# Broadcast and score products on all 128 rows of the array instead of 32 or 64, in a two-layer SSD / attention / gMLP block

## The chip, the cores and the metric

The kernel runs on one core of one Trainium2 chip. The metric is the device time of one execution in microseconds, lower is better. The kernel before was run three times: 1681.04, 1684.17 and 1684.0 us, median 1684.0 us.

## The reference, cut to what matters

Two layers work on 256 context tokens and 256 latent tokens of 1024 features. Each layer makes one wide input projection and feeds three branches with it: a bidirectional state space scan (SSD, 16 heads in four groups), an attention (8 heads of 64) and a gated MLP over tokens. Their gated sum goes through an output projection, and a SwiGLU FFN follows. The second layer computes the context only as far as the latents need it. The two places that matter here:

```python
seg = a_cum[:, :, :, None] - a_cum[:, :, None, :]
decay_ls = jnp.exp(jnp.where(tri, seg, -jnp.inf))
...
q, k = rmsnorm(q, q_norm), rmsnorm(k, k_norm)
s = jnp.einsum('bqhd,bkhd->bhqk', q, k) * (Dh ** -0.5)
```

So each SSD head needs, for each of two directions, a matrix of differences of cumulated decays between tokens, and each attention head needs scores of normalized q and k.

## The kernel before, in words

All products are made with float32 operands cut into a high part in the short TensorE format (F32R) and a low part that holds the rest. A product of a weight with activations is three TensorE products, high by high, high by low, low by high (`mm3`, line 250). `gemm` (line 255) makes one tile of 128 features that way, 24 products for 1024 input features. Weights stream from memory in tiles of 128 x 1024; ScalarE (ACT) makes the high part (line 226) and VectorE (DVE) the low part (line 236), at most two tiles ahead of TensorE (`LA`, line 41).

The order of all work is written by hand. `tick` (line 314) is called by the products with weights and lets the side work of three queues go on: the SSD's (`ssd`), attention's and the MLP's (`att`), and the conditioning vectors' (`mod`). Each `yield` in a side generator is a place where the products with weights go on. TensorE takes its instructions in that order. PSUM has eight banks of 512 columns (`S`, line 119), and 61 buffers of 128 x 512 serve nearly all intermediate tiles (`T`, line 116).

The places that the change touches:

- `decay` (line 902). For one head, one stream and each direction, a product spreads one row of `R` over all partitions: the stationary operand is a column of `sel` (minus one where the row index is the wanted one), repeated 128 times. `R` has 128 rows: for each of the two streams 64, namely the high parts of two directions times 16 heads and then their low parts. The product takes only the 64 rows of its own stream (`p`, line 905) and 384 columns. A second product (line 910) adds a mask in bfloat16 with the identity `idb` as stationary operand and `mfb` moving, on 128 rows. A call makes two such pairs.
- `carried` (line 952). For a pair of heads, a product with `selp` spreads rows of `RA` over 64 partitions each; it takes 32 rows, those of the group, and 512 columns.
- `qk_norm` (line 1008). The inverse norms `RQ` of the heads are spread in the same way, 32 rows for each of four pairs of heads (line 1035).
- `product` (line 1071). The scores of one head are two products: `Q` (high part of q, twice, one above the other) with `K` (high and low part of k), on 128 rows, and `lo` (low part of q) with the high part of k, on the head's own 64 rows.
- `stack` (line 1044) prepares Q, K and `lo` of a head, at least one step of `attention` before its scores.
- The constants: `cst`, `sel`, `selp`, `mfb` (lines 129 to 150, 608 to 619).

```python
p = slice(0, 64) if last else slice(64 * s_, 64 * s_ + 64)
mm(ps[:, 0:384], sel[p, d * 16 + hd:d * 16 + hd + 1].to_broadcast([64, 128]),
   Rt["R"][p, (128, 0)[d]:(512, 384)[d]], True, False)
...
mm(pa, selp[32 * g:32 * g + 32, pr].rearrange("k a b -> k (a b)"), Rt["A"][32 * g:32 * g + 32, :])
...
mm(ps, Q[:, q0:q0 + 128], K[:, 0:n], True, False)
mm(ps, lo[p, q0:q0 + 128], K[p, 0:n], False, True)
```

Of the kernel before, what the change touches and what calls it, by code (L numbers as in the profile page):

```python
# [9 lines left out]
F32 = mybir.dt.float32  # L10
# [15 lines left out]
# columns of the parameter pack  # L26
# [3 lines left out]
# columns of the constant pack  # L30
C_GT, C_LE, C_LT, C_GE, C_ONE, C_ID, C_MF, C_MB = (128 * i for i in range(8))
C_COS = 1024
C_SIN = 1280
C_ROW = 1536
C_BS = 1568
C_SP = 1600
NC_ = 1604
# [58 lines left out]
def kernel(ctx: ExitStack, tc: tile.TileContext, a, out):  # L96
# [31 lines left out]
    # ------------------------------------------------------------------ constants  # L128
    cst = cpool.tile([128, NC_], F32, name="cst")
    csil = cpool.tile([128, 2, D], F32, name="csil")  # L130
    csT = cpool.tile([128, 8, 32], F32, name="csT")
# [9 lines left out]
    epsb = cpool.tile([128, 1], F32, name="epsb")  # L141
    DVE.memset(epsb, EPS)
    eps4 = cpool.tile([128, 1], F32, name="eps4")
    DVE.memset(eps4, 4.0 * EPS)
    eps64 = cpool.tile([128, 1], F32, name="eps64")
    DVE.memset(eps64, 64.0 * EPS)
    idb = cpool.tile([128, 128], BF16, name="idb")
    mfb = cpool.tile([128, 256], BF16, name="mfb")
    sel = cpool.tile([128, 32], F32R, name="sel")
    selp = cpool.tile([128, 2, 2, 64], F32R, name="selp")  # L150
# [7 lines left out]
    # ------------------------------------------------------------------ adaLN vectors  # L158
# [22 lines left out]
    def mod_gen(items):  # L181
        """items: (layer, group of eight feature tiles, both streams)"""
# [23 lines left out]
    # ------------------------------------------------------------------ weight stream  # L206
# [48 lines left out]
    def gemm(acts, c0, c1=512, la=LA):  # L255
        """one tile of 128 features"""
        nk = len(acts)
        ps = S("g")
        for k, (ah, al, b) in enumerate(acts):
            wh, wl = ws.get(pos[0] + k, la=la)  # L260
            mm3(ps[:, c0:c1], wh, wl, ah[:, c0 - b:c1 - b], al[:, c0 - b:c1 - b], k == 0, k == nk - 1)
            if k % KT == KT - 1 or k == nk - 1:
                tick((k % KT + 1) / 4 * (c1 - c0) / 512)
        pos[0] += nk
        return ps

    def gemm_group(acts, nk, n, ranges, kmajor, pl=None, tk=True):
        """n tiles of 128 features, k outside, one range of tokens after the other"""
# [13 lines left out]
    # ------------------------------------------------------------------ side work  # L282
# [19 lines left out]
    def later(dt, fn):  # L302
        """emits fn when the tensor engine has been given dt more"""
        if dt:
            pending.append((now[0] + dt, fn))
        else:
            fn()
# [6 lines left out]
    def tick(f=1.0):  # L314
        """f: share of twelve passes over 512 tokens that the tensor engine has just been given"""
# [29 lines left out]
    def table(func):  # L345
        """loads the function's table ahead of its use"""
        ACT.activation(dummy, epsb, func)

    # ------------------------------------------------------------------ norms over features
    class SumSq:  # L350
# [21 lines left out]
        def root(self, c0, c1, scale, bias):  # L372
            """1 / sqrt(scale * sum + bias), with tokens on partitions"""
# [9 lines left out]
        def spread(self, c0, c1):  # L383
            """... and on all partitions (in PSUM)"""
# [6 lines left out]
    class MakeH:  # L391
        """the modulated norm of one range of tokens, one tile after the other; hi and lo start at column b"""
# [4 lines left out]
        def to(self, k):  # L397
            """emits all tiles up to k"""
# [20 lines left out]
    class Scaled:  # L419
        """the latents of x times A with the shift as two more columns: products with it need no norm yet"""  # L420
# [27 lines left out]
        def norm(self, ps):  # L448
            """(product without the shift's part, the shift's part)"""
# [5 lines left out]
    # ------------------------------------------------------------------ start  # L455
# [7 lines left out]
    for i0, i1 in ((C_ONE, C_MF), (C_ROW, C_BS)):  # L463
        SP.dma_start(out=cst[:, i0:i1], in_=a["cst"][:, i0:i1])
# [27 lines left out]
    def start_rows(k):  # L492
        """shift and scale of 128 features"""
# [9 lines left out]
    def start_mod(k):  # L503
        """... with features on partitions, and h of these features"""
# [16 lines left out]
    # the first product runs along, its operands' features outside  # L521
# [38 lines left out]
    x = None  # L560
# [6 lines left out]
    # ================================================================== layers  # L567
    for l in range(NL):
# [8 lines left out]
        # tanh(x / 2) stands for the sigmoids  # L577
        DVE.tensor_scalar(pcol(P_BG, 120), pcol(P_BG, 120), 0.5, None, MUL)

        # ---------------- gMLP: u with features on partitions, v with tokens on partitions  # L580
# [27 lines left out]
        if not last:  # L608
            SP.dma_start(out=cst[:, 0:C_ONE], in_=a["cst"][:, 0:C_ONE])
            SP.dma_start(out=cst[:, C_MF:C_ROW], in_=a["cst"][:, C_MF:C_ROW])  # L610
            SP.dma_start(out=cst[:, C_BS:NC_], in_=a["cst"][:, C_BS:NC_])
            DVE.tensor_copy(idb, ident)
            DVE.tensor_copy(mfb, cst[:, C_MF:C_MF + 256])
            DVE.tensor_scalar(sel, cst[:, C_ROW:C_ROW + 32], -1.0, None, MUL)
            DVE.tensor_copy(selp, cst[:, C_SP:C_SP + 4].rearrange("p (a b) -> p a b", a=2).unsqueeze(3).to_broadcast(
                [128, 2, 2, 64]))
            # -1 where the rows of lo are
# [3 lines left out]
        def token_major(n0, evac, between=()):  # L621
            """256 columns of the projection with tokens on partitions; others' tiles between"""
# [44 lines left out]
        # ---------------- convolution: B 8..11, C 12..15, xs 0..7  # L667
        Bt, Ct, xs = [], [], []

        def conv(ps, m, b0):  # L670
            """half of the five taps' sum, then silu; m: tile of the convolution's channels"""
# [43 lines left out]
        def dt_gemm():  # L715
            """four column tiles at once, each with a quarter of the features"""
# [17 lines left out]
        Rt = {}  # L734

        def dt_gen():
# [18 lines left out]
            # log1p(e) = 2 atanh(e / (2 + e))  # L755
# [19 lines left out]
            # by token: sums over the tokens of a tile that follow or precede, and over all of them  # L775
# [10 lines left out]
            # -F and -G of each token, relative to the middle of the sequence: [tile, stream, twice, direction, head]  # L786
            s0 = 1 if last else 0
            for i in (0, 1):
# [3 lines left out]
            # decays to the context's ends  # L792
# [4 lines left out]
            # decays from the context's ends to the latents: [direction, tile, (group, twice, head, -)]  # L797
# [15 lines left out]
            # by row: hi of direction and head, then lo; each tile of tokens twice  # L813
            ps, pa = S(), S()
            m = 64 if last else 128
            for i in (0, 1):
                PE.transpose(ps[0:m, i * 128:i * 128 + 128],
                             nF[:, i, s0:].rearrange("p s r d h -> p (s r d h)"), ident)
# [6 lines left out]
            ACT.copy(R4[0:m], twice(ps[:, 0:256], slice(0, m)))  # L825
            ACT.copy(RA, pa)
            yield
            for p0 in range(32, m, 64):
# [6 lines left out]
        # ---------------- SSD, one group of four heads at a time  # L835
# [9 lines left out]
        def ssd_group(g):  # L845
            streams = (1,) if last else (0, 1)
            xa, xb = xs[2 * g], xs[2 * g + 1]
            # context: tokens on partitions, x (256 columns) and B (128)
# [28 lines left out]
            # the context's end states  # L877
# [24 lines left out]
            def decay(s_, hh):  # L902
                """exp(F_l - F_s) and exp(G_l - G_s) of one head, masked: [s0 l0 | s0 l1 | s1 l1], [s0 l0 | s1 l0 | s1 l1]"""
                hd = 4 * g + hh
                p = slice(0, 64) if last else slice(64 * s_, 64 * s_ + 64)
                pf, pb = S(), S()
                for d, ps in ((0, pf), (1, pb)):
                    mm(ps[:, 0:384], sel[p, d * 16 + hd:d * 16 + hd + 1].to_broadcast([64, 128]),
                       Rt["R"][p, (128, 0)[d]:(512, 384)[d]], True, False)
# [10 lines left out]
            def weights(s_, hd, ef, eb):  # L920
                """W[s, l] of one head, both directions"""
# [5 lines left out]
                # s in tile 0  # L927
                STT(W[:, 128:256], ef[:, 128:256], df(0), c[:, 128:256], MUL, MUL)
                DVE.tensor_scalar(eb[:, 0:128], eb[:, 0:128], db(0), None, MUL)
                # s in tile 1  # L930
# [8 lines left out]
            def yout(s_, pr, W, ex):  # L939
                """y of a pair of heads, in the place of xs"""  # L940
# [11 lines left out]
            def carried(pr):  # L952
                """what the context's end states add to the latents of a pair of heads"""
                pa, pc = S(), S()
                mm(pa, selp[32 * g:32 * g + 32, pr].rearrange("k a b -> k (a b)"), Rt["A"][32 * g:32 * g + 32, :])
# [35 lines left out]
        # ---------------- q and k, attention  # L991
# [3 lines left out]
        def qk_tile(j, kind):  # L995
            """j: pair of heads"""
# [11 lines left out]
        def qk_norm(kind):  # L1008
            """one over the root of each head's mean square; q's with the scores' factor of 1/8"""
# [17 lines left out]
            # rows of hi, then of lo  # L1027
# [4 lines left out]
            for j in range(4):  # L1032
                ps = S()
                p = slice(32 * j, 32 * j + 32)
                mm(ps[:, b:], selp[p, 0].rearrange("k a b -> k (a b)"), RQ[p, b:])
# [5 lines left out]
        def attention():  # L1041
            st = {}

            def stack(hd):
                """hi of q twice, hi over lo of k (or lo over hi), and lo of q"""
# [4 lines left out]
                st[hd] = Q, lo, K, p  # L1050
# [20 lines left out]
            def product(ps, hd, q0, n):  # L1071
                Q, lo, K, p = st[hd]
                mm(ps, Q[:, q0:q0 + 128], K[:, 0:n], True, False)
                mm(ps, lo[p, q0:q0 + 128], K[p, 0:n], False, True)
# [44 lines left out]
            def transp(s_, pr):  # L1119
                """P with keys on partitions: [key, key tile, query]"""  # L1120
# [59 lines left out]
        def vg_half(half):  # L1180
            def ev(i, o):
# [4 lines left out]
                elif last:  # L1186
                    # the context's h, for the tiles that follow
# [19 lines left out]
        # ---------------- convolution of one group, other tiles while the group's arithmetic goes on  # L1207
# [23 lines left out]
        # ---------------- gated branches  # L1231
# [17 lines left out]
        def gated_branch(br, acts, first, lag, ready=None, done=None):  # L1249
            """gate tiles, and branch tiles lag behind them"""  # L1250
# [15 lines left out]
        # ---------------- gate and norm of the SSD branch  # L1266
# [10 lines left out]
        def ssd_norm():  # L1277
            yield
            yield
            # z carries a factor of two  # L1280
# [18 lines left out]
        # ---------------- projection of the SSD branch  # L1299
# [14 lines left out]
        # ---------------- output projection and residual  # L1314
# [309 lines left out]
```

## Time and profile before

| | before |
|---|---|
| median of three runs (1681.04 to 1684.17) | 1684.0 us |
| span of the profiled execution, first to last instruction | 1679.5 us |
| the profiled execution's own time | not told apart from the three; 1.5 to 4.7 us above the span by them |
| TensorE busy (products) | 1668.5 us, 99% of the span |
| VectorE busy | 1161.1 us, 69% |
| ScalarE busy | 789.9 us, 47% |
| GpSimd busy | 0.2 us |
| granted TensorE clock, mean | 0.996 of full speed |

How to read the rows: PE is TensorE's product, PEld its load of the stationary operand, DVE VectorE, ACT ScalarE, POOL GpSimd. `s<-R,sel` names the tile written, then the moving and the stationary operand; `64*128 64x384` is 64 rows by 128 columns of the array and 384 moving columns. Ends of products are modelled, so a duration of 0.39 us says little; the distance from one start to the next tells how fast TensorE goes. Products of plain float32 operands (for instance `state`, `W`, `pt`) appear as two instructions each.

### The profile page before, as it was taken

What the parts mean: (1) busy time and instruction counts of PE and PEld (TensorE: products, weight loads), DVE (VectorE), ACT (ScalarE), POOL (GpSimd) and SP (SyncE); (2) the same over time, 40 slices, a digit from 0 to 9 for tenths busy, and PEclk for the clock granted to TensorE, in tenths of its full rate; (3) what the DMA queues carried; (4) which work ended last, traced back from release to release, by engine and by line L of the source; (5) the groups of instructions that cost most, each with busy time, mean ns of one, the idle gap of its engine ahead of it and who ended that gap; (6) DMA issues with size and microseconds to landing.
All of it is one profiled execution on the core that took longest, in us unless ns stands there. A gap on an engine that the chain in (4) does not pass through costs nothing.

```text
span 1679.5 us, 24795 instructions
## 1 busy us (share of the span) xinstructions
PE 1668.5 (99%) x9578; PEld 1378.1 (82%) x9578; DVE 1161.1 (69%) x2206; ACT 789.9 (47%) x1411; POOL 0.2 (0%) x4
## 2 busy tenths in 40 slices
PE   8999999999999999999999999999999999999999
PEld 5877677767678888888888888887777889999999
DVE  4377788768785865676666655778887887686553
ACT  3456554544653323432222212657455685465442
POOL 0000000000000000000000000000000000000000
PEclk8999999999999999999999999999999999999999
DMA  9412111123233445444556775433222345645553
GB/s 360 152 63 90 62 51 64 51 88 126 82 107 125 151 148 178 145 149 165 165 167 203 253 241 181 162 100 101 76 76 100 110 144 173 209 156 189 188 171 132
DMA packets 77157, 237.45 MB, mean 141 GB/s; under 512 B 9072, under 2 KB 17008, under 8 KB 76912
## 3 DMA queue, kind: packets, MB, share of 16 engines
q1 hardware_dynamic: 77040, 235.88, 41.9%
q8 instruction: 75, 1.23, 0.3%
q14 instruction: 42, 0.34, 0.1%
HBM read 231.65 MB, written 4.19 MB: 140 GB/s over the span
## 4 chain that ended last, share of the span: by engine, by line
PE 93%; DVE 3%; DMA 2%; ACT 1%; issue 1%; SPq 0%; DVEq 0%; ACTq 0%
PE g L126 77%; PE s L126 13%; DMA wm<-in_wmod 1%; PE s L1128 1%; DVE lo L236 1%; ACT hi L226 1%; DVE scr L196 0%; DMA x<-in_xT 0%; PE s L855 0%; PE rs L126 0%; DMA pv<-in_pv 0%; DVE xbc L682 0%; DVE xm L1330 0%; PE s L863 0%; SPq L461 0%
## 5 line engine op out<-in xcount | busy, mean ns | idle before, releaser
L126 PE MATMUL g<-hh,hi 128*128 128x512 f32 (+1 forms) x1280 | 474.6, 371 | 0.0
L126 PE MATMUL g<-hl,hi 128*128 128x512 f32 (+1 forms) x1280 | 461.7, 361 | 0.0
L126 PE MATMUL g<-hh,lo 128*128 128x512 f32 (+1 forms) x1280 | 461.6, 361 | 0.0
L236 DVE TENSOR_TENSOR lo<-wr,hi 128x1024 fp32r<-128x1024 f32 x316 | 381.3, 1219 | 100.9 <-ACT hi L226 100.7
L226 ACT CAST hi<-wr 128x1024 fp32r<-128x1024 f32 x316 | 322.5, 1046 | 37.8 <-DMA wr<-in_ws 34.9
L126 PEld LDWEIGHTS g<-hh,hi 128*128 128x128 f32 x1280 | 241.9, 189 | 51.6 <-issue 14.6
L126 PEld LDWEIGHTS g<-hh,lo 128*128 128x128 f32 x1280 | 241.6, 189 | 37.3
L126 PEld LDWEIGHTS g<-hl,hi 128*128 128x128 f32 x1280 | 241.9, 189 | 34.4 <-DVE hl L410 0.3
L196 DVE SCALAR_TENSOR_TENSOR scr<-wm,csil 128x1024 bf16<-128x1024 f32 x128 | 156.2, 1220 | 57.2 <-DMA wm<-in_wmod 57.1
L126 PE MATMUL g<-hp,hi 128*128 128x256 f32 x608 | 109.5, 283 | 0.0
L682 DVE SCALAR_TENSOR_TENSOR xbc<-g,pv,xbc 128x508 f32<-128x508 f32 (+3 forms) x128 | 91.3, 713 | 13.3 <-ACT xbc L676 10.1
L126 PEld LDWEIGHTS g<-hp,hi 128*128 128x128 f32 x608 | 94.8, 192 | 0.0
L126 PE MATMUL g<-hp,lo 128*128 128x256 f32 x304 | 86.2, 284 | 0.8 <-DVE lo L236 0.8
L1237 ACT ACTIVATE th<-g,pv 128x512 f32<-128x512 f32 (+1 forms) x48 | 28.0, 582 | 102.3 <-PE g L126 99.4
L126 PE MATMUL g<-fh,lo 128*128 128x512 f32 x176 | 68.6, 390 | 0.6 <-DVE lo L236 0.6
L126 PE MATMUL g<-fl,hi 128*128 128x512 f32 x176 | 68.5, 389 | 0.0
L126 PE MATMUL g<-fh,hi 128*128 128x512 f32 x176 | 68.5, 389 | 0.0
L337 ACT CAST fh<-f 128x512 fp32r<-128x512 f32 x22 | 13.6, 620 | 112.4 <-DVE f L1387 112.4
L126 PE MATMUL g<-hi,hh 128*128 128x256 f32 x224 | 64.7, 289 | 0.2 <-ACT hi L226 0.2
L126 PE MATMUL g<-lo,hh 128*128 128x256 f32 x224 | 63.6, 284 | 1.1 <-DVE lo L236 1.1
L1387 DVE TENSOR_TENSOR f<-s,g 128x256 f32<-128x256 f32 (+1 forms) x41 | 22.6, 551 | 60.7 <-PE g L126 60.3
L126 PE MATMUL g<-fp,hi 128*128 128x256 f32 x352 | 63.4, 283 | 0.0
(321 smaller groups left out, 2811.9 us busy)
## 6 DMA issues: line engine op xcount, KB each, us to landing
wr<-in_ws SPq DMA_DIRECT2D x316, 512.0 KB, 3.9
wm<-in_wmod SPq DMA_DIRECT2D x80, 512.0 KB, 4.3
wm<-in_wm SPq DMA_DIRECT2D x32, 256.0 KB, 5.8
bias<-in_rpb SPq DMA_DIRECT2D x32, 128.0 KB, 2.1
x<-in_xT SPq DMA_DIRECT2D x8, 256.0 KB, 5.2
xm<-in_xT SPq DMA_DIRECT2D x8, 256.0 KB, 6.0
xmid<-xm SPq DMA_DIRECT2D x8, 256.0 KB, 4.6
xr<-xmid SPq DMA_DIRECT2D x8, 256.0 KB, 5.3
```

The lines of the kernel that those rows point to most:

```text
L126: PE.matmul(o, l, r, start=start, stop=stop)
L196: DVE.scalar_tensor_tensor(scr, raws[n], 1.0, csil[:, v, :], MUL, MUL, accum_out=modr[l][:, ft, v:v + 1])
L226: ACT.copy(hi, self.raw[i])
L236: DVE.tensor_tensor(lo, self.raw.pop(i), hi, SUB)
L337: ACT.copy(hi, src[:, c0:])
L682: DVE.scalar_tensor_tensor(av3[:, :, o0:o1], pv3[:, :, o0 + d:o1 + d], w(j), av3[:, :, o0:o1], MUL, ADD)
L1128: PE.transpose(ps[:, kt * 256 + qt * 128:kt * 256 + qt * 128 + 128], src, ident)
L1237: ACT.activation(th[:, c0:], ps[:, c0:], AF.Tanh, scale=0.5, bias=pcol(P_BG + br * 8 + m))
L1387: DVE.tensor_tensor(t[:, r0:r1], s[:, r0:r1], pb[:, r0:r1], MUL)
```

## The change

The products with 32 or 64 rows take all 128 rows; zeros in the stationary operand stand for the rows that aren't wanted. For that, `sel` gets 64 columns (a half for each stream), `selp` 8 x 128 columns, `lo` is filled with zeros in the other half of its rows by GpSimd, and the second layer's `nF` is filled with zeros for the stream that it lacks, so that its transposes and `R` have 128 rows too. Some constants move: the masks to a tile of the general buffers, the transposed conditioning vectors `csT` too, and three small constants into one tile. Comments are removed in many places. The diff, cut to what acts:

```diff
-    csT = cpool.tile([128, 8, 32], F32, name="csT")
+    csT = T("csT")[:, 0:256].rearrange("p (k v) -> p k v", v=32)
...
-    sel = cpool.tile([128, 32], F32R, name="sel")
-    selp = cpool.tile([128, 2, 2, 64], F32R, name="selp")
+    sel = cpool.tile([128, 64], F32R, name="sel")
+    selp = cpool.tile([128, 8, 128], F32R, name="selp")
...
-            SP.dma_start(out=cst[:, C_MF:C_ROW], in_=a["cst"][:, C_MF:C_ROW])
-            SP.dma_start(out=cst[:, C_BS:NC_], in_=a["cst"][:, C_BS:NC_])
+            SP.dma_start(out=cst[:, C_COS:C_ROW], in_=a["cst"][:, C_COS:C_ROW])
+            SP.dma_start(out=cst[:, C_BS:C_MF], in_=a["cst"][:, C_BS:C_MF])
+            masks = T("masks")
+            SP.dma_start(out=masks[:, 0:256], in_=a["cst"][:, C_MF:NC_])
             DVE.tensor_copy(idb, ident)
-            DVE.tensor_copy(mfb, cst[:, C_MF:C_MF + 256])
-            DVE.tensor_scalar(sel, cst[:, C_ROW:C_ROW + 32], -1.0, None, MUL)
-            DVE.tensor_copy(selp, cst[:, C_SP:C_SP + 4].rearrange("p (a b) -> p a b", a=2).unsqueeze(3).to_broadcast(
-                [128, 2, 2, 64]))
+            DVE.tensor_copy(mfb, masks[:, 0:256])
+            for s_ in (0, 1):
+                DVE.tensor_scalar(sel[:, s_ * 32:s_ * 32 + 32], cst[:, C_ROW:C_ROW + 32],
+                                  cst[:, C_BS + s_:C_BS + s_ + 1], -1.0, MUL, MUL)
+            DVE.tensor_copy(selp.rearrange("p a (b c) -> p a b c", c=64),
+                            cst[:, C_SP:C_SP + 16].rearrange("p (a b) -> p a b", b=2).unsqueeze(3).to_broadcast(
+                                [128, 8, 2, 64]))
...
+        def pair_rows(j, pr):
+            return selp[:, 2 * j + pr]
...
+            if last:
+                nc.gpsimd.memset(nF[:, :, 0], 0.0)
...
-            m = 64 if last else 128
             for i in (0, 1):
-                PE.transpose(ps[0:m, i * 128:i * 128 + 128],
-                             nF[:, i, s0:].rearrange("p s r d h -> p (s r d h)"), ident)
+                PE.transpose(ps[:, i * 128:i * 128 + 128],
+                             nF[:, i].rearrange("p s r d h -> p (s r d h)"), ident)
...
-            ACT.copy(R4[0:m], twice(ps[:, 0:256], slice(0, m)))
+            ACT.copy(R4, twice(ps[:, 0:256], slice(0, 128)))
...
-            for p0 in range(32, m, 64):
+            for p0 in range(32 + 64 * s0, 128, 64):
...
-                p = slice(0, 64) if last else slice(64 * s_, 64 * s_ + 64)
                 pf, pb = S(), S()
                 for d, ps in ((0, pf), (1, pb)):
-                    mm(ps[:, 0:384], sel[p, d * 16 + hd:d * 16 + hd + 1].to_broadcast([64, 128]),
-                       Rt["R"][p, (128, 0)[d]:(512, 384)[d]], True, False)
+                    c = s_ * 32 + d * 16 + hd
+                    mm(ps[:, 0:384], sel[:, c:c + 1].to_broadcast([128, 128]),
+                       Rt["R"][:, (128, 0)[d]:(512, 384)[d]], True, False)
...
-                mm(pa, selp[32 * g:32 * g + 32, pr].rearrange("k a b -> k (a b)"), Rt["A"][32 * g:32 * g + 32, :])
+                mm(pa, pair_rows(g, pr), Rt["A"])
...
-                p = slice(32 * j, 32 * j + 32)
-                mm(ps[:, b:], selp[p, 0].rearrange("k a b -> k (a b)"), RQ[p, b:])
+                mm(ps[:, b:], pair_rows(j, 0), RQ[:, b:])
...
-                st[hd] = Q, lo, K, p
+                st[hd] = Q, lo, K
+                nc.gpsimd.memset(lo[o, c0:].bitcast(F32), 0.0)
                 ACT.copy(K[p], k[p])
...
-                Q, lo, K, p = st[hd]
+                Q, lo, K = st[hd]
                 mm(ps, Q[:, q0:q0 + 128], K[:, 0:n], True, False)
-                mm(ps, lo[p, q0:q0 + 128], K[p, 0:n], False, True)
+                mm(ps, lo[:, q0:q0 + 128], K[:, 0:n], False, True)
...
-    for v in range(4):
-        c[:, C_SP + v] = (i % 32 < 8) & (i % 4 == v)
+    for v in range(16):
+        c[:, C_SP + v] = (i // 32 == v // 4) & (i % 32 < 8) & (i % 4 == v % 4)
```

## Rows read from the trace of the kernel before

**Rows 1.** The page: span, and busy time of the engines.

```profile
span 1679.5 us, 24795 instructions
...
PE 1668.5 (99%) x9578; PEld 1378.1 (82%) x9578; DVE 1161.1 (69%) x2206; ACT 789.9 (47%) x1411; POOL 0.2 (0%) x4
```

**Rows 2.** The page: the chain that ended last, by engine.

```profile
PE 93%; DVE 3%; DMA 2%; ACT 1%; issue 1%; SPq 0%; DVEq 0%; ACTq 0%
```

**Rows 3.** The tiles R, RA, RQ, ql: their products; count, shortest, median, longest ns.

```profile
L126 PE MATMUL s<-R,sel x96: 434/438/439, 165.4 to 1307.4; 64*128 64x384 f32 x96
L126 PE MATMUL s<-RA,selp x16: 489/496/498, 189.6 to 1308.0; 32*128 32x512 f32 x16
L126 PE MATMUL s<-RQ,selp x16: 377/496/500, 185.0 to 1269.9; 32*128 32x512 f32 x12, 32*128 32x256 f32 x4
L126 PE MATMUL s<-ks,ql x48: 379/492/502, 395.0 to 1370.1; 64*128 64x512 f32 x32, 64*128 64x256 f32 x16
```

**Rows 4.** The chain in order of time, two stretches without side work: start, length, what.

```profile
532.44 163.25 PE g L126 x720
1400.96 66.97 PE g L126 x558
```

**Rows 5.** Timeline around one call of decay, first layer: start, length, engine, what.

```profile
165.12 0.39 PE L126 MATMUL g<-hh,lo 128*128 128x512 f32 x1
165.44 0.18 PEld L126 LDWEIGHTS s<-R,sel 64*128 64x128 f32 x1 [0.35 <-issue]
165.44 0.44 PE L126 MATMUL s<-R,sel 64*128 64x384 f32 x1
...
165.81 0.28 PE L126 MATMUL s<-mfb,idb 128*128 128x256 bf16 x1
166.02 0.43 PE L126 MATMUL s<-R,sel 64*128 64x384 f32 x1
166.39 0.28 PE L126 MATMUL s<-mfb,idb 128*128 128x256 bf16 x1
166.43 0.48 PE L126 MATMUL g<-hh,hi 128*128 128x512 f32 x1
166.51 0.19 PEld L126 LDWEIGHTS g<-hl,hi 128*128 128x128 f32 x1
166.74 0.39 PE L126 MATMUL g<-hl,hi 128*128 128x512 f32 x1
```

**Rows 6.** Timeline of TensorE where products on 64 columns precede decay.

```profile
243.89 1.08 PE L126 MATMUL s<-W,xt 128*64 128x256 f32 x8
244.90 0.44 PE L126 MATMUL s<-R,sel 64*128 64x384 f32 x1
```

**Rows 7.** The chain in order of time, one head of the second layer's attention.

```profile
1343.22 1.51 PE s L126 x4
1344.73 3.07 PE g L126 x24
```

**Rows 8.** Windows of 20 us: busy us of PE, PEld, DVE, ACT, POOL.

```profile
245.00:265.00 20.00, 20.00 (x83) 13.29 (x83) 19.13 (x49) 10.70 (x24) 0.00 (x0) 1.00 0.13 43
465.00:485.00 20.00, 20.00 (x105) 14.01 (x103) 18.69 (x42) 13.75 (x32) 0.00 (x0) 1.00 0.41 137
1320.00:1340.00 20.00, 20.00 (x138) 16.79 (x135) 18.91 (x44) 13.26 (x28) 0.00 (x0) 1.00 0.38 129
1340.00:1360.00 20.00, 20.00 (x140) 16.15 (x139) 19.29 (x51) 18.16 (x41) 0.00 (x0) 1.00 0.38 122
```

**Rows 9.** Timeline: a weight tile's low part, and the first product that reads it.

```profile
1347.55 1.22 DVE L236 TENSOR_TENSOR lo<-wr,hi 128x1024 fp32r<-128x1024 f32 x1
...
1351.88 0.28 PE L126 MATMUL g<-hh,lo 128*128 128x256 f32 x1
```

**Rows 10.** Timeline of VectorE behind the first layer's constants, and its idle time there.

```profile
55.55 0.29 DVE L615 CAST selp<-cst 128x256 fp32r<-128x256 f32 x1
...
58.82 3.50 DVE L236 TENSOR_TENSOR lo<-wr,hi 128x1024 fp32r<-128x1024 f32 x3 [2.73 <-ACT hi L226]
```

More of the change, by code (lines that the diff above doesn't have):

```diff
@@ L29 @@
 NPV = 206
[L31 to L37, printed above, removed]
+C_GT, C_LE, C_LT, C_GE, C_ONE, C_ID = (128 * i for i in range(6))
+C_COS = 768
+C_SIN = 1024
+C_ROW = 1280
+C_BS = 1312
+C_SP = 1344
+C_MF = 1360
+C_MB = 1488
+NC_ = 1616
 N_T = 61
@@ L126, in mm @@
         PE.matmul(o, l, r, start=start, stop=stop)
-    cst = cpool.tile([128, NC_], F32, name="cst")
+    cst = cpool.tile([128, C_MF], F32, name="cst")
     csil = cpool.tile([128, 2, D], F32, name="csil")
-    csT = cpool.tile([128, 8, 32], F32, name="csT")
+    csT = T("csT")[:, 0:256].rearrange("p (k v) -> p k v", v=32)
     scr = cpool.tile([128, D], BF16, name="scr")
@@ L139, in load_params @@
         SP.dma_start(out=rw[l], in_=a["rows"][l])
[L141 to L146, printed above, removed]
+    eps3 = cpool.tile([128, 3], F32, name="eps3")
+    epsb, eps4, eps64 = (eps3[:, i:i + 1] for i in range(3))
+    for e, f in ((epsb, 1.0), (eps4, 4.0), (eps64, 64.0)):
+        DVE.memset(e, f * EPS)
     idb = cpool.tile([128, 128], BF16, name="idb")
     mfb = cpool.tile([128, 256], BF16, name="mfb")
-    sel = cpool.tile([128, 32], F32R, name="sel")
-    selp = cpool.tile([128, 2, 2, 64], F32R, name="selp")
+    sel = cpool.tile([128, 64], F32R, name="sel")
+    selp = cpool.tile([128, 8, 128], F32R, name="selp")
     lom = cpool.tile([128, 1], F32, name="lom")
@@ L462 @@
         x.append(t)
-    for i0, i1 in ((C_ONE, C_MF), (C_ROW, C_BS)):
+    for i0, i1 in ((C_ONE, C_COS), (C_ROW, C_BS)):
         SP.dma_start(out=cst[:, i0:i1], in_=a["cst"][:, i0:i1])
@@ L559 @@
     ws.ahead = 3
-    x = None
+    x = csT = None
     xmid = dpool.tile([128, 8, TOK], F32, name="xmid")
```

## The prediction

> **What bounds the kernel now.** I read the page first: TensorE is busy for 1668.5 of 1679.5 us [rows 1], and the chain that ended last is TensorE's own for 93% [rows 2]. A busy TensorE needn't be at its peak, since ends are modelled; so I compared starts. In the chain, where only products with weights run, 720 of them with 512 columns take 163.25 us and 558 with 256 columns 66.97 us [rows 4]: 0.227 and 0.120 us from one start to the next, the pace of the full array. Then I looked for places slower than that, and the timeline shows them at the products that the change widens.
>
> Around one call of `decay` [rows 5], the product before R starts at 165.12. R starts 0.32 us later (0.227 at pace), and its weight load starts with it, not ahead. The mask product comes 0.37 us after R (384 columns; between the two paces I estimate 0.173). So a product on 64 rows costs about 0.09 us on the way in and 0.20 on the way out. On full rows it is otherwise: the load for `hl,hi` starts at 166.51, 0.08 us after its preceding product's start, and lies under it.
>
> **The change part by part, in time of this execution** (span 1679.5 us; the median of the runs is 4.5 us above it, and I keep that distance).
>
> *Decay.* From 165.12 to 166.74 the call takes 1.62 us [rows 5]. At full pace it would be two products of 512, two of 384 and two of 256 columns: 2 x 0.227 + 2 x 0.173 + 2 x 0.120 = 1.04 us. The mask is in bfloat16; I price it like the other 256 columns. So 0.58 us a call, 0.29 a narrow product. There are 96 narrow products, 48 calls [rows 3]: 27.8 us. In twelve of the calls (counted in TensorE's timeline) products on 64 columns come just before [rows 6]; that switch stays, so I take 0.20 us off each: 2.4. Left: 25.4 us.
>
> *Scores.* Four products and the 24 that follow take 1.51 + 3.07 = 4.58 us in the second layer [rows 7]. At pace, 4 x 0.227 + 24 x 0.120 = 3.79. That is 0.79 us a head, 0.40 per `ql` product, more than in decay, since the next float32 load is exposed too. 48 of them [rows 3]: 19.1 us.
>
> *`RA` and `RQ`.* 32 products on 32 rows [rows 3]. Bounds: 0.29 us as in decay, 0.40 as in the scores. What follows them is float32 as in the scores, so 0.40: 12.7 us.
>
> Sum: 25.4 + 19.1 + 12.7 = 57 us of TensorE time, all on the path, because TensorE is the path [rows 2].
>
> *What is added.* `selp` is built four times as wide, `sel` in two pieces; a row of 1024 columns costs VectorE 1.2 us at most (three in 3.50 us [rows 10]), and behind the constants VectorE sits idle for 2.73 us waiting for ScalarE's high part [rows 10]: nothing, and at most 1 us without that cover. One more small load stands in SP's queue ahead of the second group of constants' users: nothing, as these are read much later. The second layer's full transposes and copies of `nF`: under 1 us, left out. Sixteen fills of `lo` on GpSimd, one per head and layer, and two small ones: GpSimd works 0.2 us in the whole span [rows 1], so nothing is queued behind them. The trace shows no fill of this size on it; the cost is nothing as long as one is shorter than a head's step, over 4.58 us [rows 7], because `stack` comes at least a step before the scores; beyond that TensorE waits for it.
>
> *What is late next.* VectorE has to do the same work in less time. In four windows of 20 us it is busy for 18.7 to 19.3 [rows 8], so idle 0.9, 1.3, 1.1 and 0.7. TensorE would save there, by the narrow products in each: 245 to 265 seven R, two RA, one RQ, 3.2 us; 465 to 485 seven `ql`, 2.8; each of the two in the second layer six `ql`, 2.4. Above VectorE's idle time that is 2.3 + 1.5 + 1.3 + 1.7 = 6.8 us. Part of it is covered by VectorE's lead: a weight tile's low part made at 1348.77 is first read at 1351.88, 3.1 us later [rows 9]. From none to 6.8 lost, I take 5, nearer the upper end, as in the second layer's attention three heads' savings (2.4 us) nearly use up that lead.
>
> So 57 - 5 = 52 us: the span goes to 1627.5 us, the time from 1684 to **1632 us**.
>
> **The rivals.**
> *VectorE takes over.* Where it is over 93% busy [rows 8], its low parts and softmax work set the pace and attention's whole 19.1 us are given back, besides the 5: 57 - 24 = 33, 1651 us. For it: those windows. Against it: the lead of 3.1 us [rows 9] and lighter windows between. Chance 0.10.
>
> *The switch to bfloat16 is what costs.* After R comes the mask in bfloat16, and no row shows float32 before bfloat16 on full rows. If the 0.20 us on the way out belong to that switch, 96 x 0.20 = 19 us stay: again 33 us, 1651. Against it: the way back, mask to `hh,hi` to `hl,hi`, takes 0.35 us (166.39 to 166.74 [rows 5]), just 0.120 + 0.227; and the scores, with no bfloat16, show the same price. Chance 0.09.
>
> *The wide loads stay exposed, and the change does nothing.* Then each wide product waits for its load as the narrow one does: 1684. Against it: loads on full rows start under the product before [rows 5]. The Trainium skill, "TensorE: Matmul & The Clock Gate", Part 3, The mechanism, has a rule for this rival: a weight load passes running products only if its row group is another one or it goes to the background buffer, and the list What overlaps and what doesn't below it names the row group alone. By that list the change would gain nothing; the load at 166.51 speaks for the background buffer. Chance 0.02.
>
> *The narrow products run beside others.* Then a wide one costs its whole length: 96 x 0.173 + 60 x 0.227 + 20 x 0.120 = 33 us more, 1717. Against it: after R the next product starts 0.37 us later, more than its whole length at pace [rows 5]. The Trainium skill, "TensorEngine Tiling (Array Packing)", When to Use Tiling, speaks for this rival: it advises two or four row tiles for a contraction of 64 or 32. The gaps in the trace don't bear it out here, where hardly any narrow product has another beside it. Chance 0.01.
>
> *GpSimd's fills are late: slower.* In `stack`, the fill now stands between a buffer's release and the scores. If one took 10 us, each of 16 heads would wait 10 - 4.6 = 5.4 us: 86 lost against 57 gained, 1713. It decides from 4.6 + 57 / 16 = 8.2 us a fill. For it: no row has its price. Against it: VectorE writes 1024 columns in 1.2 us [rows 10], and GpSimd has nothing else to do. Chance 0.02.
>
> **How the numbers follow.** The forecast keeps 0.76. Faster by over 0.2% (3.4 us, about what a measurement of this kernel can tell): forecast, VectorE and bfloat16, 0.95; same 0.02; slower 0.03. The range: below, nothing lost on VectorE and the twelve switches gone too, 57 + 2.4 = 59.6, and the runs' own spread of 3 us: 1621. Above, 1651 of the two larger rivals with 5 us more lost: 1656. That leaves out 0.05 and the mis-sizing of what I estimated.
>
> **What would show it.** R, RA, RQ and `ql` appear with 128 rows. Right: R starts 0.23 us after a 512-column product, the mask 0.17 after R; four score products take about 0.9 us; TensorE stays over 98% busy and the stretches without side work [rows 4] keep their length. VectorE's share rises to about 1161 / 1628 = 71%. Wrong: the mask still 0.37 us after R (bfloat16); waits of TensorE for `lo` or for the softmax's tiles between 1270 and 1340 of the new span (VectorE); waits for a fill of `lo` (GpSimd). A saving below 33 us would mean that the price of the switch isn't in the narrow rows.

## The result, and the profile after

The changed kernel takes 1632.46 us (median of four runs, 1631.14 to 1635.84) against 1683.8 us for the kernel before in the same comparison: a ratio of 0.9701 [0.9688, 0.9715]. Timed again later, it took 1633.52 us against 1682.45: 0.9713 [0.97, 0.9726]. The forecast was 1632. The profiled execution took 1635.84 us with a span of 1634.0.

The page of the kernel after: span, busy time of the engines, and the chain that ended last by engine.

```profile
span 1634.0 us, 24855 instructions
...
PE 1619.0 (99%) x9578; PEld 1373.7 (84%) x9578; DVE 1160.1 (71%) x2207; ACT 787.5 (48%) x1411; POOL 7.0 (0%) x21
...
PE 86%; DVE 7%; DMA 3%; ACT 2%; issue 1%; SPq 0%; ACTq 0%; DVEq 0%
```

TensorE has as many products as in [rows 1], and is busy for 49.5 us less. The other engines do the same work in less time. The chain is no longer TensorE's for 93% [rows 2]: VectorE has 7% of it instead of 3.

The four tiles in the kernel after: products, with shortest, median and longest ns.

```profile
L129 PE MATMUL s<-R,sel x96: 338/418/740, 171.6 to 1266.8; 128*128 128x384 f32 x96
L129 PE MATMUL s<-RA,selp x16: 474/477/480, 192.1 to 1267.1; 128*128 128x512 f32 x16
L129 PE MATMUL s<-RQ,selp x16: 278/473/579, 188.5 to 1231.8; 128*128 128x512 f32 x12, 128*128 128x256 f32 x4
L129 PE MATMUL s<-ks,ql x48: 278/392/398, 379.3 to 1324.9; 128*128 128x512 f32 x32, 128*128 128x256 f32 x16
```

The same counts as in [rows 3], all on 128 rows: the change does what it says. Their durations fell by far less than was gained, since ends are modelled; the starts tell more. The timeline around a call of `decay` in the kernel after, to be laid beside [rows 5]:

```profile
171.34 0.39 PE L129 MATMUL g<-hh,lo 128*128 128x512 f32 x1
171.34 0.19 PEld L129 LDWEIGHTS s<-R,sel 128*128 128x128 f32 x1
171.56 0.34 PE L129 MATMUL s<-R,sel 128*128 128x384 f32 x1
...
171.74 0.28 PE L129 MATMUL s<-mfb,idb 128*128 128x256 bf16 x1
171.78 0.42 PE L129 MATMUL s<-R,sel 128*128 128x384 f32 x1
172.04 0.28 PE L129 MATMUL s<-mfb,idb 128*128 128x256 bf16 x1
172.08 0.48 PE L129 MATMUL g<-hh,hi 128*128 128x512 f32 x1
172.40 0.39 PE L129 MATMUL g<-hl,hi 128*128 128x512 f32 x1
```

From 171.34 to 172.40 the call takes 1.06 us, where it took 1.62. R starts 0.22 us after the product ahead, the mask 0.18 after R. The load of R's stationary operand now starts with the product before it instead of behind it. (A start in bfloat16 stands 0.04 us ahead of the next one here, 171.74 and 171.78; such pairs are read as a sum.)

The chain of the kernel after in the second layer's attention, and the long stretch behind:

```profile
1306.41 1.23 DVE lo L237
...
1316.44 0.50 ACT pt L1142
...
1317.64 0.92 PE s L129 x4
1318.56 2.85 PE g L129 x24
...
1355.54 66.97 PE g L129 x558
```

Four scores and the 24 products behind them take 0.92 + 2.85 = 3.77 us, where [rows 7] has 4.58 and the forecast 3.79. The stretch without side work keeps its 66.97 us to the digit [rows 4]. But the two rows at the top are new: the kernel before has only TensorE in its chain through this attention; now VectorE, and behind it ScalarE, stand in the chain in front of TensorE.

**Where the time went, by stretch.** From the starts of the first product of chosen weight tiles in TensorE's timeline, in us (before, after, and five of the kernels of the experiments below):

```
                     before  after  all_narrow  narrow_decay  narrow_pairs  narrow_scores  after_again
opening               85.92  92.08       88.10         90.16         87.23          88.12        89.19
SSD, 1st layer       220.04 198.18      220.19        214.18        203.54         198.17       198.17
attention, 1st       149.63 140.24      149.67        140.24        140.23         149.68       140.23
SSD, 2nd layer       170.46 156.24      170.48        164.26        162.00         156.22       156.24
attention, 2nd        63.24  58.96       63.25         58.95         58.95          63.25        58.91
```

SSD's two stretches gain 21.9 + 14.2 us, attention's two 9.4 + 4.3, together 49.8. The remaining stretches between and behind these agree within 0.1 us, but for one in the middle (between the first layer's attention and the second's SSD, some 620 us) that lies between 617.3 and 620.2 us in the traces, whichever kernel. The opening (until the first convolution's products) got longer, by 6.2 us in this profiled execution; 3.9 of that lie in its first 60 us, which vary by 6 us over the traces, from 2.1 less to 3.9 more than before, and 2.25 behind them (see "The opening").

### The profile page after: what moved, and what is told of

Its sections match the earlier page's. It is cut to its first block, busy times and chain, and to the rows that moved or that the text cites. A ratio compares the mean times of both kernels' runs of the same rounds, so it can differ in the third digit from the quotient of the medians.

```text
span 1634.0 us, 24855 instructions
## 1 busy us (share of the span) xinstructions
PE 1619.0 (99%) x9578; PEld 1373.7 (84%) x9578; DVE 1160.1 (71%) x2207; ACT 787.5 (48%) x1411; POOL 7.0 (0%) x21
## 4 chain that ended last, share of the span: by engine, by line
PE 86%; DVE 7%; DMA 3%; ACT 2%; issue 1%; SPq 0%; ACTq 0%; DVEq 0%
PE g L129 75%; PE s L129 10%; DMA wm<-in_wmod 2%; DVE lo L237 2%; PE s L1140 1%; DVE xbc L689 1%; ACT hi L227 1%; DVE scr L197 1%; DVE bt L1095 0%; DMA x<-in_xT 0%; DVE ks L1068 0%; DMA xr<-xmid 0%; PE s L867 0%; PE rs L129 0%; DMA pv<-in_pv 0%
## 5 line engine op out<-in xcount | busy, mean ns | idle before, releaser
L129 PE MATMUL g<-hi,hl 128*128 128x256 f32 x224 | 64.0, 286 | 0.0
```

The costliest lines, as they stand in the source:

```text
L129: PE.matmul(o, l, r, start=start, stop=stop)
```

## The experiments

Twelve runs. The leading theory was the prediction's: a lone product on part of the rows costs 0.29 to 0.40 us beyond its own length. Rivals were the step to bfloat16, VectorE and GpSimd.

**Each part put back alone.** `narrow_decay` makes R's products on 64 rows again, in an otherwise changed kernel:

```diff
-                    mm(ps[:, 0:384], sel[:, c:c + 1].to_broadcast([128, 128]), Rt["R"][:, ...
+                    p = slice(64 * s_, 64 * s_ + 64)
+                    mm(ps[:, 0:384], sel[p, c:c + 1].to_broadcast([64, 128]), Rt["R"][p, ...
```

> The changed kernel (1632.5 us) with decay's 96 products back on 64 rows, all else wide. Theory (a price for each switch between full and partial rows, 0.09 us in and 0.20 us out): 25.4 us come back, 1658 us, a little less where VectorE held TensorE up in the changed kernel; the mask comes 0.37 us after R again. Rival (the switch between float32 and bfloat16 costs): the wide form pays it too, so hardly anything comes back, 1632 to 1636 us.

Measured: 1657.07 us, 0.9853 [0.9839, 0.9868]. By the table against `after_again`, 16.0 + 8.0 = 24.0 us came back, all in SSD. Its timeline around the call (TensorE's products):

```profile
169.42 0.39 PE L129 MATMUL g<-hh,lo 128*128 128x512 f32 x1
169.74 0.44 PE L129 MATMUL s<-R,sel 64*128 64x384 f32 x1
170.11 0.28 PE L129 MATMUL s<-mfb,idb 128*128 128x256 bf16 x1
170.32 0.44 PE L129 MATMUL s<-R,sel 64*128 64x384 f32 x1
170.69 0.28 PE L129 MATMUL s<-mfb,idb 128*128 128x256 bf16 x1
170.73 0.47 PE L129 MATMUL g<-hh,hi 128*128 128x512 f32 x1
171.04 0.39 PE L129 MATMUL g<-hl,hi 128*128 128x512 f32 x1
```

With 64 rows the call is back at 1.62 us (169.42 to 171.04), and the mask at 0.37 us behind R. The mask is bfloat16 in both kernels; only the rows differ. So the 0.20 us on the way out belong to the narrow rows, not to the step to bfloat16. Over all 48 calls, by starts against `after_again`, 36 lose about 0.57 us and one 0.50; the eleven that follow directly on products with 64 columns lose 0.37 to 0.39.

`narrow_scores` and `narrow_pairs` do the same for the scores and for `RA` and `RQ`:

```diff
-                mm(ps, lo[:, q0:q0 + 128], K[:, 0:n], False, True)
+                mm(ps, lo[p, q0:q0 + 128], K[p, 0:n], False, True)
```

> The changed kernel with the 48 third score products back on 64 rows (the fills of lo stay). Theory: TensorE loses 19.1 us again, but in the changed kernel it waits about 4.7 us in the two attentions for VectorE's softmax and low parts (3.1 us in the first layer, 1.6 in the second), and these waits go away: 1632.5 + 19.1 - 4.7 = 1647 us. Rival (VectorE didn't cost anything, the price of a score product was under-sized): 1651 us or more.

Measured: 1645.85 us, 0.9787 [0.9772, 0.9801]. By stretches 9.45 + 4.34 = 13.8 us came back.

```diff
-                mm(pa, pair_rows(g, pr), Rt["A"])
+                mm(pa, selp[32 * g:32 * g + 32, 2 * g + pr], Rt["A"][32 * g:32 * g + 32, :])
...
-                mm(ps[:, b:], pair_rows(j, 0), RQ[:, b:])
+                mm(ps[:, b:], selp[32 * j:32 * j + 32, 2 * j], RQ[32 * j:32 * j + 32, b:])
```

> The changed kernel with the 32 broadcasts of RA and RQ back on 32 rows. Theory: 0.40 us each, 12.7 us back, 1645 us. Lower bound of the forecast, 0.29 us each: 1642 us. If only the first product after the switch matters and these products hide beside decay's, less than 5 us.

Measured: 1644.14 us, 0.9781 [0.9765, 0.9797]; 5.4 + 5.8 = 11.1 us by stretches. What one such product costs shows in the starts around it. `narrow_pairs`, then the kernel after, TensorE's products in the first layer:

```profile
187.55 0.28 PE L129 MATMUL s<-mfb,idb 128*128 128x256 bf16 x1
187.76 0.50 PE L129 MATMUL s<-RA,selp 32*128 32x512 f32 x1
188.19 1.13 PE L129 MATMUL s<-xbc,state 128*128 128x256 f32 x4
```

```profile
192.03 0.28 PE L129 MATMUL s<-mfb,idb 128*128 128x256 bf16 x1
192.07 0.48 PE L129 MATMUL s<-RA,selp 128*128 128x512 f32 x1
192.38 1.02 PE L129 MATMUL s<-xbc,state 128*128 128x256 f32 x4
```

From the mask to the product behind RA 0.64 us became 0.35: 0.29 saved, as in `decay`. But the four products behind it took 1.13 us and now take 1.02, so another 0.11 goes with the narrow product. Together it is 0.40, the price that I had taken. By the starts of all 32 in `narrow_pairs` and `after_again`, 26 cost 0.37 to 0.41 us; the shortfall against 12.7 comes from the other six. Four RA cost 0.22 to 0.28, one RQ behind products on 64 columns 0.19, and before one RQ the wide kernel waits for VectorE (0.18 us idle in the trace), so that the narrow one is even 0.19 quicker there.

**All three put back.** `all_narrow` keeps only the constants, fills and moved tiles of the change.

> The changed kernel with all three kinds back on 32 and 64 rows; constants, masks, csT, the fills and the full transposes of nF stay as changed. Theory: the narrow rows are all of it, so the time of before, 1684 us within 2 us. Rival (moved constants, the general buffers or the fills carry part of the change): off from 1684 us by more than 3 us, either way.

Measured: 1683.77 us (ten runs) against 1681.65 (thirteen): 1.0015 [1.0005, 1.0024]. So these edits aren't free: they cost about 2 us. By the table it is the opening, 88.10 against 85.92. That was not in the prediction, and became a question of its own (below).

**Does the count of narrow products matter, or that of the switches?** `adjacent_narrow` changes the kernel *before*: within a call of `decay` both products R come first, and then both masks, so the same 96 narrow products stand in pairs.

```diff
                 for d, ps in ((0, pf), (1, pb)):
                     mm(ps[:, 0:384], sel[p, ...
+                for d, ps in ((0, pf), (1, pb)):
                     mm(... mfb ...
```

> The kernel before with the four products of a decay call in another order: both R products, then both masks, so that the two products on 64 rows stand side by side. Theory (a price for each switch): one switch in and out a call instead of two, 48 x 0.29 = 14 us less than before, a ratio near 0.992, and the second R follows the first after about 0.17 us. Rival (a price for each narrow product, whatever stands beside it): no change, ratio 1.000.

Measured: 1666.47 us against 1680.89, 0.9911 [0.9897, 0.9925]. Its timeline of TensorE around the call:

```profile
167.06 0.39 PE L126 MATMUL g<-hh,lo 128*128 128x512 f32 x1
167.37 0.61 PE L126 MATMUL s<-R,sel 64*128 64x384 f32 x2
167.92 0.39 PE L126 MATMUL s<-mfb,idb 128*128 128x256 bf16 x2
168.07 0.47 PE L126 MATMUL g<-hh,hi 128*128 128x512 f32 x1
168.38 0.39 PE L126 MATMUL g<-hl,hi 128*128 128x512 f32 x1
```

From 167.06 to 168.38 it is 1.32 us, 0.30 less than before: a pair of narrow products costs what one alone costs, with not one row more used. 48 calls x 0.30 = 14.4 us, and the stretches of SSD gave 9.6 + 4.8. The order also halves the steps between float32 and bfloat16, but the kernel after has all of these and takes 1.06 us a call, so they are not what is saved. So the price is not one for each narrow product, whatever stands beside it; a price for each switch between row shapes, there and back, gives the total.

One expectation was a miss: the second R was to follow the first after 0.17 us, and it follows after 0.28 in all 48 calls; the mask then comes 0.27 us behind it (167.92) instead of 0.37. So the price of the pair is spread over three steps, of about 0.1 us each over pace. Why the step between two products of one shape isn't free, no run shows.

**Is attention's missing part VectorE's?** `zero_low` leaves out the third score term's content: `lo` is filled with zeros whole, and VectorE's subtraction for it is gone; TensorE's products stay.

```diff
-                nc.gpsimd.memset(lo[o, c0:].bitcast(F32), 0.0)
+                nc.gpsimd.memset(lo[:, c0:].bitcast(F32), 0.0)
...
-                    DVE.tensor_tensor(lo[p, c0:], q[p, c0:], Q[p, c0:].bitcast(F32), SUB)
```

> The changed kernel without VectorE's 16 subtractions that make the low part of q (0.42 to 0.69 us each); lo is filled with zeros whole instead, so the third score term is left out of the result while its product still runs. Theory (VectorE holds TensorE up in the attentions): VectorE is freed of 9 us there, and of TensorE's 4.7 us of waits 2 to 4 go: 1628 to 1630 us. Rival (the waits are latency of the chain through ScalarE, not VectorE's load): within 1 us of the changed kernel.

Measured: 1628.89 us, 0.9686 [0.9673, 0.97]. Attention's stretches are shorter by 1.73 and 1.80 us than in `after_again`: less work for VectorE makes TensorE faster there; SSD's stretches keep their length within 0.04 us. The rest of the 4.6 us between the two times is not told apart from the spread of the opening and the middle. The places show in the kernel after, first layer, in its timeline:

```profile
429.74 0.39 PE L129 MATMUL g<-hh,lo 128*128 128x512 f32 x1
430.26 0.93 DVE L1126 TENSOR_SCALAR pc<-pc,ast 128x256 f32<-128x256 f32 x2
...
431.08 0.71 PE L1140 MATMUL s<-cst,pc 128*128 128x128 f32 x4 [0.96 <-DVE pc L1126]
```

TensorE stands idle for 0.96 us until VectorE has normalized the softmax. In all, the profile has TensorE wait 2.7 us in the two attentions of `after_again`: 2.4 for VectorE's tiles (`pc`, `bt`, `z`), 0.3 for ScalarE's copy `pt`, none for `ql` itself, so the shorter chain to the scores is not what `zero_low` wins. Of these waits 0.7 us, for `pc`, are left in it. And in windows of 20 us (busy us of PE, PEld, DVE, ACT, POOL) the kernel after has, in the second layer's attention:

```profile
1300.00:1320.00 20.00, 19.03 (x141) 16.55 (x140) 19.28 (x49) 18.69 (x42) 0.65 (x3) 1.00 0.45 133
```

VectorE's 19.28 is about what the densest window of [rows 8] had (19.29), but now TensorE is at 19.03 instead of 20.00.

`pool_low` gives that subtraction to GpSimd:

```diff
-                    DVE.tensor_tensor(lo[p, c0:], q[p, c0:], Q[p, c0:].bitcast(F32), SUB)
+                    nc.gpsimd.tensor_tensor(lo[p, c0:], q[p, c0:], Q[p, c0:].bitcast(F32), SUB)
```

> The changed kernel with these 16 subtractions on GpSimd instead of VectorE, same result. Theory: VectorE is freed as in zero_low, so 2 to 4 us faster than the changed kernel, 1628 to 1630 us, unless GpSimd is so slow that the scores wait for it, or slows VectorE's own work beside it; then 1632 us or more.

Measured: 1633.18 us, 0.9708 [0.9695, 0.9721], no different from `after_again`; attention's stretches took 140.46 and 58.86 us. GpSimd's subtractions in `pool_low` for the second layer (busy us, mean ns), then VectorE's other subtraction from 1285 to 1340, in that layer's attention, first in `after_again`, then in `pool_low`:

```profile
L1069 POOL TENSOR_TENSOR ql<-q,qs 64x256 fp32r<-64x256 f32 x8 | 7.4, 930 | 40.4 <-ACT qs L1064 35.8 <-DVE bt L1104 4.6
```

```profile
L1068 DVE TENSOR_TENSOR ks<-k,ks 64x512 fp32r<-64x512 f32 x6 | 4.1, 686 | 0.2
```

```profile
L1068 DVE TENSOR_TENSOR ks<-k,ks 64x512 fp32r<-64x512 f32 x6 | 6.7, 1112 | 0.2
```

GpSimd does it in 930 ns (the first layer's, of 64 x 512, in 1390), and VectorE's own subtraction, begun meanwhile, takes 1112 ns instead of 686: in that window 2.6 us are lost on VectorE, as much as six subtractions of 64 x 256 (420 ns each) had cost it. The Trainium skill, "SBUF — State Buffer", section "SBUF: two separate sides", says that an instruction of VectorE with two SBUF inputs and one of GpSimd that reads SBUF shut each other out, for the whole of the one that starts first. The trace agrees: each of the six began 0.28 to 0.42 us behind GpSimd's subtraction and ended 0.55 us behind that one's end, and two of the first layer, begun 0.1 and 0.57 us ahead of GpSimd's, kept their 685 to 687 ns.

**Do the fills cost?** `double_fill` fills `lo`'s other half twice, on GpSimd.

> The changed kernel with each fill of lo on GpSimd made twice (about 0.4 us more for each of 16). Theory (fills are covered by GpSimd's idle time and come a head's step ahead): no change, 1632 us within 1 us. Rival (the scores wait for the fills): 16 x 0.4 = 6 us more, 1639 us.

Measured: 1634.41 us, 0.9719 [0.9706, 0.9733]; no stretch of SSD or attention moves by over 0.4 us. The fill's group in the kernel after:

```profile
L1062 POOL MEMSET ql<- 64x512 f32 x8 | 4.2, 521 | 434.6 <-DVE W L948 367.3 <-PE s L1140 14.8 <-DVE ast L1123 13.6
```

0.52 us a fill (0.31 in the second layer), far from the 8.2 us from which it would have decided.

**The opening.** Timeline of ScalarE, from 52 to 62 us: before, `all_narrow`, and `early_table`, the kernel made for it.

```profile
53.84 1.28 ACT L606 ACT_TABLE_LOAD   x1
55.22 2.64 ACT L606 ACTIVATE u<-g 128x512 f32<-128x512 f32 x4
```

```profile
55.21 1.28 ACT L607 ACT_TABLE_LOAD   x1 [1.38 <-PE g L129]
56.50 2.07 ACT L607 ACTIVATE u<-g 128x512 f32<-128x512 f32 x4
```

```profile
55.03 1.28 ACT L348 ACT_TABLE_LOAD   x1
56.33 0.20 ACT L348 ACTIVATE dummy<-eps 128x1 f32<-128x1 f32 x1
56.44 2.56 ACT L609 ACTIVATE u<-g 128x512 f32<-128x512 f32 x4
```

Before, the table of the gelu is loaded while TensorE still works on its input. In `all_narrow` (and after) the load itself sits idle for 1.38 us until TensorE's tile is there, and comes 1.4 us later. In the kernel before, too, a wait of the activation stands in front of the load, but one that was over at 52.3 us; in `all_narrow` it is the wait for TensorE's tile, over at 55.2. My reading, argued only: `csT` now takes one of the general buffers, so `u` falls on a buffer with another former user and its activation has other waits. TensorE then waits for the next weight tile, whose parts come later, first in `all_narrow`, then in `early_table`:

```profile
59.54 0.38 PE L129 MATMUL g<-hi,hh 128*128 128x256 f32 x1 [0.95 <-ACT hi L227]
60.80 0.40 PE L129 MATMUL g<-lo,hh 128*128 128x256 f32 x1 [0.88 <-DVE lo L237]
```

```profile
59.99 0.38 PE L129 MATMUL g<-hi,hh 128*128 128x256 f32 x1 [0.20 <-ACT hi L227]
```

The second wait is 0.88 us in `early_table` too (before: 0.19 and 0.87). The next windows (60 to 70 us; the number behind the five busy times is the granted clock, of full speed) in `all_narrow` and in `early_table`:

```profile
60.00:70.00 10.00, 9.20 (x64) 9.20 (x65) 3.02 (x3) 2.04 (x4) 0.00 (x0) 0.83 0.49 159
```

```profile
60.00:70.00 10.00, 9.12 (x74) 8.93 (x75) 3.46 (x3) 2.48 (x4) 0.00 (x0) 1.00 0.48 159
```

With the two long pauses, one product between them, the granted clock fell to the lower level (1.2 of 2.4 GHz) for a part of the window, 64 products instead of 74; with one long pause it stayed at 1.00. `early_table` loads the table by a dummy activation ahead of the first `u`:

```diff
         u = []
+        if not last:
+            table(AF.Gelu_apprx_tanh)
         for i in range(4):
```

> The changed kernel with ScalarE's table for gelu loaded by a dummy activation ahead of the first u. In the changed kernel (and with all rows narrow again) the load starts only behind the wait for TensorE's first tile, 1.4 us later than before, the next weights' high part is 0.7 us late, TensorE stands still for 1.1 instead of 0.35 us, and its clock is granted at half for a stretch of 3.4 us soon after. Theory: this is what made the all-narrow kernel 2.5 us slower than before; 2.2 us faster than the changed kernel, about 1631 us where that is 1633, and the stretch from the first tile of v to the first convolution takes 28.8 us as before instead of 31.1. Rival (the late table is not the cause): the same as the changed kernel.

Measured: 1632.55 us, 0.9708 [0.9695, 0.9722]. From the first product of the third branch of the opening to the first convolution it takes 28.87 us: before 28.86, `all_narrow` and `after_again` 31.1. So the stretch is mended. Other traces bear it out: it takes 31.0 to 31.1 us in all ten with the late load, and 28.9 in the four with an early one (before, `adjacent_narrow`, `early_table`, `early_and_late`). The whole time is not told apart from the kernel after: the opening as a whole varies by more (85.9 to 92.1 us), and in this execution the stretch in the middle was 2.2 us longer than in `after_again`, with the clock at 0.84 for one window of 10 us.

**A try to win the waits back.** `late_transposes` makes attention's transposes a step later, to give VectorE more time; `early_and_late` adds the early table.

```diff
-A_T = (2, 2)
+A_T = (3, 3)
```

> The changed kernel with attention's transposes of the weights one step later (A_T 3 instead of 2), so that VectorE's softmax has a step more. Theory (TensorE waits for VectorE's normalised weights ahead of the transposes): in the first layer most of the 3.0 us of waits go; in the second VectorE has as much work as before and TensorE then waits for low parts instead, 0 to 1 us gained. Together 2 to 4 us faster, 1629 to 1631 us. Rival (VectorE is the bound over the whole stretch, or more live tiles bring other waits): within 1 us of the changed kernel.

> Both: the early table and the later transposes. Theory: the two gains add up, 4 to 6 us faster than the changed kernel, 1627 to 1629 us, ratio to before 0.967 to 0.969.

Measured: 1641.25 us, 0.9761 [0.9748, 0.9775], and 1638.65 us, 0.9746 [0.9733, 0.9759]: both a miss: the first is about 8 us slower than the kernel after, the second 6 us slower than `early_table`. The timeline of `late_transposes`:

```profile
397.07 0.65 PE L129 MATMUL s<-pt,va 128*64 128x256 f32 x2
...
400.21 0.65 PE L129 MATMUL s<-pt,va 128*64 128x256 f32 x4 [2.48 <-ACT pt L1142]
```

The products with v stay at step 4, so only one step is left for ScalarE to copy the transposes out of PSUM, behind its other work in order; TensorE waits for that copy for up to 2.48 us at a time, 5.1 us in the first layer. I moved the wait from VectorE to ScalarE and made it longer. The early table made 2.6 us of difference between these two; by the traces 2.2 of it lie in the opening, where it works, but attention and the middle differ as well.

No version clearly beats the changed kernel with the same computation.

## Why the prediction was right

- **What bounds it, and where the slow places are.** Right. Starts at the pace of the full array were the measure, and the changed products came to it: 1.06 us a call against 1.04, 3.77 us a head against 3.79. The unchanged stretches did not move.
- **Decay, 25.4 us.** 24.0 came back with the narrow rows. The call saves 0.56 instead of 0.58 us: 48 x 0.56 - 2.4 = 24.5. The calls behind products on 64 columns are eleven by the trace, not twelve, and save about 0.2 us less each, as taken.
- **`RA` and `RQ`, 12.7 us.** 11.1. "So 0.40" held for 26 of the 32, the product behind counted in (0.37 to 0.41). The other six make the average 0.35; among them one RQ behind products on 64 columns, which I had discounted for `decay` only, and one at which VectorE is waited for.
- **Scores, 19.1 us, and 5 lost on VectorE.** The net 14.1 measured 13.8. Where nothing waits, a head saves the 0.8 us forecast; the rest, 19.1 - 13.8 = 5.3 us, is lost in the attentions (some 0.5 less by the 0.39 us a product that the starts show). `zero_low`, with some of VectorE's work gone, wins 3.5 of them back, which shows that these are VectorE's; the others are argued. That the 5 fits so well is partly luck: of the 6.8 us behind it, 2.3 lay in a window of SSD, where the kernel after has one wait for VectorE, of 0.18 us.
- **"What is added ... nothing."** This step failed. VectorE's cover and GpSimd's fills held, but I had not costed what moves between the pools. It costs about 2 us in the opening (`all_narrow`): a table load that lost its lead, and a stretch at half clock behind. That the table load is the cause is shown by `early_table` (28.87 us against 31.1); that it is late because `csT` shifts the buffers is argued only.
- **The sum.** The gain was 51.3 us in the first comparison and 48.9 in the second, where 52 was forecast. By the stretches it was 49.8 - 2, some 4 us less than forecast. So it is partly luck that 1632 fell so near: three of the four runs of before in the first comparison are those I started from, and later ones were 1 to 3 us faster (medians 1680.89 to 1682.45).

**The rivals.** VectorE does not take over: attention loses about 5 us, not all of its 19.1. The switch to bfloat16 fell with `narrow_decay`. The wide loads are not exposed: the load at 171.34 starts together with the running product. The list in the Trainium skill, "TensorE: Matmul & The Clock Gate", Part 3, What overlaps and what doesn't, by which a load passes only on another row group, is not what this trace shows; both stand on all rows here. That narrow products run beside others fell too: taking them away gained instead of costing 33 us. And the total of `adjacent_narrow`, 0.30 us less a call with half the switches, agrees with a sentence that I had not used: the Trainium skill, "TensorEngine Tiling (Array Packing)", Key Properties, says that a change of tiling mode, not merely of tile, drains TensorE. The 0.11 us over pace between two products of one shape it leaves open. GpSimd's late fills fell with 0.52 us a fill.

## What to carry to other kernels

A lone product on 32 or 64 rows among products on all rows costs 0.29 us here with a bfloat16 product behind it, and about 0.39 with a float32 one, more than the product itself; pad its stationary operand with zeros where the rows exist anyway, or put narrow products next to each other. Read TensorE's waste from the distance between starts and compare it with the same shape in a stretch without side work, since a busy share of 99% hid 50 us. When TensorE gets faster, look at the engine whose windows were nearly full before, and when tiles move between buffer pools, at who inherits which buffer.

## What the runs showed of the hardware that I had not expected

- Two narrow products in a row cost together what one alone costs: 0.30 us less a call, in the kernel before, though the second starts 0.28 us behind the first, not 0.17.
- A subtraction on GpSimd (64 x 256, 930 ns) slowed VectorE's own two-input subtraction (64 x 512), begun behind it, from 686 to 1112 ns.
- An activation's table load waited for the activation's input tile, 1.38 us, where before it had run ahead of it.
- Two pauses of TensorE, 0.95 and 0.88 us with one product between, went with a granted clock of 0.83 in the window behind; pauses of 0.20 and 0.88 us at the same place with 1.00.
